# A transformer block and a hybrid block on one core: ScalarE and VectorE kept in the order of emission, and a row's store put behind its sum of squares

## The chip, the core and the metric

The kernel runs on one core of one Trainium2 chip. Five engines work side by side: TensorE (PE in the profile; PEld is its weight load), VectorE (DVE), ScalarE (ACT), GpSimd (POOL) and SyncE (SP), which here mostly issues DMAs. Each engine takes its own list of instructions, and waits for the others by semaphores. The metric is the device time of one execution in microseconds (us), lower is better; the median over several runs counts.

## The reference

1024 rows of width 1024 in float32 go through two blocks.

```
# first block
x = x + 0.5 * rms_norm(swiglu(rms_norm(x), w_gate, w_up, w_down))      # FFN1, inner width 2816
x = x + rms_norm(token_mixer(rms_norm(x)))                             # 8 heads with forget gates, 4 differential heads
x = x + 0.5 * rms_norm(swiglu(rms_norm(x), w_gate, w_up, w_down))      # FFN2
# second block, on 16 learned rows + the 1024 rows
h = h + mixed(RG-LRU, SSD)(rmsnorm(h)) @ w_out                         # even layer: two recurrences with short convolutions
h = h + stick_breaking(rmsnorm(h)) @ w_out                             # odd layer: 16 heads, cumulative sums instead of softmax
return rmsnorm(h)[16:]
```

## The kernel before

**Stages.** FFN1 runs to about 700 us of the span, the mixer to 1300, FFN2 to 1990, the even layer to 2760, and the odd layer to the end. Every product is made of three passes over operands that are split into a high and a low part (`mm3`: high by high, low by high, high by low). So each operand of TensorE needs two earlier steps: ScalarE casts the high part (`wh`, `w0h`, `T`, `th`, `Ah`: a `copy` to fp32r), and VectorE subtracts it from the source for the low part (`wl`, `w0l`, `tl`, `Al`). The two FFNs use a scheme with fewer products of larger sums: VectorE forms the sums (`sg` L826, `w` L785), and `T3`, `T4` are split sums of the activations. DMAs are issued from SP's queue, and the stores of finished rows from ScalarE's queue (L607).

**Two orders.** The class `Sched` (L109 to L198) is the kernel's own planner: threads ask for time on an engine with a cost (`("A", act(n))`, `("V", dve(n))`, ...), and the thread that can start first by these costs is served, so it decides the order in which instructions are emitted. The framework below the kernel (Tile) then has a scheduler of its own, which takes ready instructions by its own estimates and may place an instruction of any engine before others that were emitted earlier. In the kernel before only loads of activation tables and the activations `act_t` are tied to each other (`pin`, `last`, `after_pin`). By count, 1141 of VectorE's instructions and 557 of ScalarE's stand directly behind one that was emitted later.

**Names of the steps below.** At the start, `Start.half` squares four rows `xr` on ScalarE for their sums (`ss`), VectorE computes 1/sqrt (`rsqrt`, 12 small operations L287 to L294) and scales the rows (`norm`, L626); TensorE transposes them (`ptf`, L577), and `Ah`, `Al` (L565) are the split of the result; `w0h`, `w0l` are the first weights. `ahead_of` (L508 on) prepares `w_out` of a later stage during FFN1: eight blocks `prer` come by DMA, are cast on ScalarE, subtracted on VectorE (L520), and go back to DRAM. In the even layer `xc` is a convolution (L2550, L2553), and L2766 to L2770 make the decay blocks `ab` of a chunk, eight small operations. In the odd layer `kt` is a scan (L2275), `pt` the weights that come from it (L2279), `th` and `tl` (L1552) the split of their transposes, which TensorE multiplies with the values into `po` (L1587). `Rows.put` takes one finished row tile: store it to DRAM, square and sum it.

Of the kernel before, what the change touches and what calls it, by code (L numbers as in the profile page):

```python
# [12 lines left out]
AF = mybir.ActivationFunctionType  # L13
# [5 lines left out]
P = 128  # L19
# [21 lines left out]
class Res:  # L41


    def __init__(self, n):
        self.free = [0.0] * n
        self.queue = []
# [50 lines left out]
def act(n):  # L97
    return 0.07 + 0.92e-3 * n
# [102 lines left out]
class Ctx:  # L201
    def __init__(self, ctx, tc):
        self.ctx = ctx
        self.tc = tc
        nc = self.nc = tc.nc
        self.sch = Sched(self.act_set)
        self.const = ctx.enter_context(tc.tile_pool(name="const", bufs=1))
        self.small = ctx.enter_context(tc.tile_pool(name="small", bufs=4))
        self.ap = ctx.enter_context(tc.tile_pool(name="act", bufs=1))
        self.wp = ctx.enter_context(tc.tile_pool(name="W", bufs=1))  # L210
        self.psp = None
        self.ahead = None
        self.dr = ctx.enter_context(tc.tile_pool(name="dr", bufs=1, space=DRAM))
        self.ident = self.const.tile([P, P], F32, name="ident")
        make_identity(nc, self.ident)
        self.eps = self.const.tile([P, 1], F32, name="epsc")
        nc.vector.memset(self.eps, EPS)
        self.one = self.const.tile([P, 1], F32, name="onec")
        nc.vector.memset(self.one, 1.0)
        self.pin = None  # L220
        self.last = None
        for nm in ("activation", "copy"):
            def f(*a, _o=getattr(nc.scalar, nm), **k):
                self.last = _o(*a, **k)  # L224
                return self.last
            setattr(nc.scalar, nm, f)
        self.onesm = self.const.tile([P, P], F32, name="onesm")
        nc.vector.memset(self.onesm, 1.0)

    def new_A(self):  # L230
        return (self.ap.tile([P, KD, L], F32R, tag="Ah", name="Ah"),
                self.ap.tile([P, KD, L], F32R, tag="Al", name="Al"))

    def after_pin(self, ins):

        if self.pin is not None:
            self.tc.add_manual_dep(ins.ins, self.pin.ins.name, mybir.DependencyInfo(
                mybir.DependencyClass.NoSync, mybir.DependencyReason.DATA), reason="table set")
        return ins

    def act_set(self, name):

        ins = self.after_pin(self.nc.scalar.preload_act_table_set(name))
        if self.last is not None and self.last is not self.pin:
            self.tc.add_manual_dep(ins.ins, self.last.ins.name, mybir.DependencyInfo(
                mybir.DependencyClass.NoSync, mybir.DependencyReason.DATA), reason="table set")
        self.pin = ins

    def act_need(self, name):

# [332 lines left out]
class Rows:  # L583
# [15 lines left out]
    def put(self, t, y, junk):  # L599

        c, g = self.c, self.GROUP[t]
        ms = self.members(t)
        if g not in self.ss:
            self.ss[g] = c.small.tile([P, len(ms)], F32, tag=f"ss{len(ms)}", name="ss", bufs=5)
        if self.dram is not None:
            r0 = self.row0 + t * P
            c.nc.scalar.dma_start(self.dram[r0:r0 + P, :], y)  # L607
        tt = yield ("A", act(1024))
        c.nc.scalar.activation(junk(), y, AF.Square, accum_out=self.ss[g][:, t - g:t - g + 1])
        self.stored[t].set(tt + 3.0)  # L610
        self.left[g] = self.left.get(g, len(ms)) - 1
        if self.left[g] == 0:
            if t >= self.tables:
                self.r[g] = yield from c.rsqrt_t(self.ss[g], 1.0 / D)
                tt = c.sch.time
            else:
                tt = yield ("V", c.RSQRT)
                self.r[g] = c.rsqrt(self.ss[g], 1.0 / D)
            for u in ms:
                self.ev[u].set(tt)  # L620
# [2688 lines left out]
```

## Time and profile before

| | |
|---|---|
| median of 3 runs (lowest to highest) | 3579.32 us (3578.43 to 3579.59) |
| the profiled execution's own time | 3577.13 us |
| its span, first to last instruction | 3575.4 us |
| TensorE busy | 3430.7 us, 96% |
| VectorE busy | 2749.9 us, 77% |
| ScalarE busy | 1700.6 us, 48% |
| mean granted TensorE clock, of full speed | 0.987 |

The profile is of one execution. [...]

### The profile page before, as it was taken

How to read it: one execution, taken by the hardware profiler on the slowest of the kernel's cores; microseconds unless marked ns; L12 is line 12 of the kernel's file. 1: busy time of each engine (PE TensorE's matmuls, PEld its weight loads, DVE VectorE, ACT ScalarE, POOL GpSimd, SP SyncE). 2: the span in 40 equal slices, each digit the busy share in tenths (PEclk: the TensorE clock that was granted, in tenths of full speed). 3: DMA queues.
4: the chain of work that ended last, by engine and by line, in shares of the span. 5: the costliest groups of instructions: out<-in, count | busy, mean ns of one | idle time of the engine just before them, and what ended most of it. 6: DMA issues, size and time to landing. Idle time of an engine off the chain costs nothing.

```text
span 3575.4 us, 51885 instructions
## 1 busy us (share of the span) xinstructions
PE 3430.7 (96%) x19675; PEld 2925.6 (82%) x19675; DVE 2749.9 (77%) x5050; ACT 1700.6 (48%) x3451; POOL 326.1 (9%) x355
## 2 busy tenths in 40 slices
PE   8999999899999999999999899998999999999998
PEld 6788888678888877888888899988878888888877
DVE  8876699988888769666799779578633688878784
ACT  5323245556666643232345447447422465656561
POOL 0111144000000001111351000000000000000000
PEclk9999999999999999999999999999999999999999
DMA  5542372311211551323552334244473110111133
GB/s 183 178 132 89 113 284 83 128 58 44 73 41 36 179 168 60 123 89 109 195 197 72 108 64 86 61 87 90 139 244 95 57 36 28 33 31 31 33 134 107
DMA packets 305842, 366.07 MB, mean 102 GB/s; under 512 B 18644, under 2 KB 221568, under 8 KB 305592
## 3 DMA queue, kind: packets, MB, share of 16 engines
q1 hardware_dynamic: 299800, 341.71, 30.7%
q10 hardware_dynamic: 5792, 21.04, 1.6%
q8 instruction: 155, 2.54, 0.3%
q14 instruction: 95, 0.78, 0.1%
HBM read 267.58 MB, written 95.13 MB: 101 GB/s over the span
## 4 chain that ended last, share of the span: by engine, by line
PE 73%; DVE 17%; ACT 4%; issue 3%; DMA 2%; SPq 0%; POOL 0%; DVEq 0%; ACTq 0%; POOLq 0%
PE pst L337 7%; PE pst L336 7%; PE pst L338 7%; PE po L1587 3%; PE pe L336 3%; PE pe L338 3%; PE pe L337 3%; DVE kt L2275 3%; PE pdn L337 2%; PE pdn L338 2%; PE pdn L336 2%; PE ptr L1607 2%; PE pwo L3100 2%; PE pwo L3101 2%; PE pwo L3102 2%
## 5 line engine op out<-in xcount | busy, mean ns | idle before, releaser
L336 PE MATMUL pe<-Ah,wh 128*128 128x260 f32 (+1 forms) x1184 | 340.6, 288 | 21.9 <-DVE sz L2601 8.2
L338 PE MATMUL pe<-Ah,wl 128*128 128x260 f32 (+1 forms) x1184 | 337.1, 285 | 0.0
L337 PE MATMUL pe<-Al,wh 128*128 128x260 f32 (+1 forms) x1184 | 336.4, 285 | 0.0
L224 ACT CAST wh<-w 128x512 fp32r<-128x512 f32 x280 | 162.1, 619 | 252.7 <-PE pst L337 160.2
L942 DVE TENSOR_TENSOR sg<-sg,pst 128x512 f32<-128x512 f32 x280 | 187.1, 684 | 104.8 <-PE pst L338 104.4
L1006 POOL TENSOR_TENSOR h<-h 128x512 f32<-128x512 f32 x88 | 136.2, 1547 | 1332.9 <-DVE h L988 1327.7
L337 PE MATMUL pst<-Al,wh 128*128 128x512 f32 x640 | 253.7, 396 | 0.0
L336 PE MATMUL pst<-Ah,wh 128*128 128x512 f32 x640 | 252.2, 394 | 0.0
L338 PE MATMUL pst<-Ah,wl 128*128 128x512 f32 x640 | 252.1, 394 | 0.0
L473 DVE TENSOR_TENSOR wl<-w,wh 128x512 fp32r<-128x512 f32 x280 | 212.0, 784 | 50.4 <-ACT wh L224 49.0
L336 PEld LDWEIGHTS pe<-Ah,wh 128*128 128x128 f32 (+1 forms) x1184 | 223.4, 189 | 26.2 <-DVE sz L2601 8.5
L337 PE MATMUL pdn<-dl,dh 128*128 128x512 f32 x592 | 230.8, 390 | 1.9 <-DVE dl L1099 1.9
L224 ACT CAST th<-ptr 128x512 fp32r<-128x512 f32 (+2 forms) x344 | 171.6, 515 | 125.4 <-PE ptr L1607 78.7
L338 PE MATMUL pdn<-dh,dl 128*128 128x512 f32 x592 | 230.3, 389 | 0.0
L1552 DVE TENSOR_TENSOR tl<-ptr,th 128x512 fp32r<-128x512 f32 (+2 forms) x344 | 197.5, 592 | 41.8 <-ACT th L224 38.4
L336 PE MATMUL pdn<-dh 128*128 128x512 f32 x592 | 229.1, 389 | 0.0
L337 PEld LDWEIGHTS pe<-Al,wh 128*128 128x128 f32 (+1 forms) x1184 | 223.0, 189 | 1.0
L338 PEld LDWEIGHTS pe<-Ah,wl 128*128 128x128 f32 (+1 forms) x1184 | 222.8, 188 | 0.8
L2275 DVE TENSOR_TENSOR_SCAN kt<-kt,onec 128x392 f32<-128x392 f32 (+5 forms) x224 | 204.2, 916 | 16.8 <-ACT kt L224 14.9
L224 ACT CAST wh<-wr 128x1024 fp32r<-128x1024 f32 (+2 forms) x116 | 119.0, 1026 | 182.7 <-PE pwo L3101 80.3
L336 PE MATMUL pst<-T,wh 128*128 128x512 f32 x480 | 187.3, 393 | 8.7 <-ACT T L224 8.7
L337 PE MATMUL pst<-T,wh 128*128 128x512 f32 x480 | 188.1, 392 | 0.4 <-DVE T L835 0.4
(550 smaller groups left out, 10023.6 us busy)
## 6 DMA issues: line engine op xcount, KB each, us to landing
hD<-h SPq DMA_DIRECT2D x22, 1792.0 KB, 8.1
w<-in_ffn_w_gate_dram SPq DMA_DIRECT2D x20, 1024.0 KB, 5.4
w<-in_ffn_w_up_dram SPq DMA_DIRECT2D x20, 1024.0 KB, 8.0
d<-hD SPq DMA_DIRECT2D x18, 1024.0 KB, 5.4
wr<-in_even_w_in_dram SPq DMA_DIRECT2D x36, 512.0 KB, 4.3
wo<-prer SPq DMA_DIRECT2D x32, 512.0 KB, 3.6
wr<-in_odd_w_in_dram SPq DMA_DIRECT2D x32, 512.0 KB, 4.3
wr<-in_w_in_dram SPq DMA_DIRECT2D x24, 512.0 KB, 3.9
```

What stands on the lines that cost most here:

```text
L224: self.last = _o(*a, **k)
L336: nc.tensor.matmul(ps, wh, xh, start=start, stop=False)
L337: nc.tensor.matmul(ps, wh, xl, start=False, stop=False)
L338: nc.tensor.matmul(ps, wl, xh, start=False, stop=stop)
L473: (nc.gpsimd if eng == "G" else nc.vector).tensor_sub(lo, raw, hi.bitcast(F32))
L942: nc.vector.tensor_add(dst, src, ps)
L1006: nc.gpsimd.tensor_sub(q[:, o], q[:, a], q[:, b_])
L1552: nc.vector.tensor_sub(tl[:rows, :n], ptr[:rows, :n], th[:rows, :n].bitcast(F32))
L1587: nc.tensor.matmul(po[:, 256 - n:256], vs, (th, tl)[w][:rows, o:o + n], start=(x == 0 and y == 0 and 0 in which), stop=(x == last and y == ...
L1607: nc.tensor.transpose(ptr[:rows, o:o + P], pts[i][:, col:col + rows], c.ident)
L2275: nc.vector.tensor_tensor_scan(rev, rev, c.one.to_broadcast([P, m]), kt[:, k0 + m:k0 + m + 1], op0=ALU.mult, op1=ALU.mult)
L3100: nc.tensor.matmul(ps[n], oh, wh[:, sl], start=(first and k == 0), stop=False)
```

## The change

Every `activation` and `copy` of ScalarE, every table load, and fourteen kinds of VectorE operation are tied to the instruction of the same engine that was emitted before, by a dependency that needs no semaphore, since both stand in one engine's list. TensorE, GpSimd and SP are not tied. In `Rows.put` the store is emitted after the Square and tied behind it. Nothing is added to or taken from the computation.

```diff
@@ class Ctx, __init__
+        self.inner = False
...
         self.pin = None
         self.last = None
-        for nm in ("activation", "copy"):
-            def f(*a, _o=getattr(nc.scalar, nm), **k):
-                self.last = _o(*a, **k)
-                return self.last
-            setattr(nc.scalar, nm, f)
+        self.tail = {}
+        self.strict = True
+
+        def record(e, ins):
+            if e == "A":
+                self.last = ins
+            if e in self.tail:
+                self.behind(ins, self.tail[e])
+            if self.strict:
+                self.tail[e] = ins
+            return ins
+
+        self.record = record
+        for e, eng, names in (("A", nc.scalar, ("activation", "copy")), ("V", nc.vector, (
+                "memset", "reciprocal", "reduce_sum", "scalar_tensor_tensor", "stream_shuffle", "tensor_add",
+                "tensor_copy", "tensor_mul", "tensor_reduce", "tensor_scalar", "tensor_sub", "tensor_tensor",
+                "tensor_tensor_reduce", "tensor_tensor_scan"))):
+            for nm in names:
+                def f(*a, _o=getattr(eng, nm), _e=e, **k):
+                    was, self.inner = self.inner, True
+                    ins = _o(*a, **k)
+                    self.inner = was
+                    return ins if was else record(_e, ins)
+                setattr(eng, nm, f)
...
+    def behind(self, ins, first):
+
+        self.tc.add_manual_dep(ins.ins, first.ins.name, mybir.DependencyInfo(
+            mybir.DependencyClass.NoSync, mybir.DependencyReason.DATA), reason="order of emission")
...
@@ act_set
-        self.pin = ins
+        self.pin = self.record("A", ins)
...
@@ Rows.put
+        tt = yield ("A", act(1024))
+        c.nc.scalar.activation(junk(), y, AF.Square, accum_out=self.ss[g][:, t - g:t - g + 1])
         if self.dram is not None:
             r0 = self.row0 + t * P
-            c.nc.scalar.dma_start(self.dram[r0:r0 + P, :], y)
-        tt = yield ("A", act(1024))
-        c.nc.scalar.activation(junk(), y, AF.Square, accum_out=self.ss[g][:, t - g:t - g + 1])
+            c.behind(c.nc.scalar.dma_start(self.dram[r0:r0 + P, :], y), c.last)
```

By count, 96 of VectorE's instructions and 2 of ScalarE's now stand directly behind one that was emitted later. In the rows below, wrapped instructions carry the wrapper's line: L224 of ScalarE before, L243 of both engines now.

The first place is ScalarE at the start of FFN1, before:

```order
L224 ACT_TABLE_LOAD
L224 ACTIVATE junk,ss<-xr 128x1024 x4
L224 CAST w0h<-wr 128x1024 x2
L224 CAST w0h<-w_139 128x1024
L224 CAST w_149<-w_139 128x1024
L224 ACTIVATE Ah<-ptf,prm_95 128x512 x4
```

And with the change:

```order
L243 ACT_TABLE_LOAD
L243 ACTIVATE junk,ss<-xr 128x1024 x2
L243 CAST w0h<-wr 128x1024 x2
L243 ACTIVATE junk,ss<-xr 128x1024 x2
L243 CAST w0h<-w_139 128x1024
L243 CAST w_149<-w_139 128x1024
L243 CAST wh<-w 128x512
L243 ACTIVATE Ah<-ptf,prm_95 128x512 x8
```

The Squares of the second two rows (`junk,ss<-xr`) moved behind the casts of the first weights `w0h`. VectorE's order moved alike: the two `w0l` and the second rsqrt chain now stand ahead of the first two scalings of rows, and the four scalings stand together.

The second place is ScalarE in FFN1 at about 100 us, where `T3_643` and `T4_901` are split sums that TensorE waits for and `prer` belongs to the preparation of `w_out`; before:

```order
L224 CAST T3_643<-sg_803 128x512
L224 CAST wh_828<-w_180 128x512
L224 CAST wh_828<-w_219 128x512
L224 CAST wh_870<-w_180 128x512
L224 CAST wh_870<-w_219 128x512
L224 CAST prer_1687<-prer_1686 128x1024
L224 CAST T3_643<-sg_848 128x512
L224 CAST wh_928<-w_180 128x512
L224 CAST wh_928<-w_219 128x512
L224 ACTIVATE sg_909<-sg_909 128x512
L224 CAST T4_901<-sg_903 128x512
L224 CAST prer_1865<-prer_1864 128x1024
```

And with the change:

```order
L243 CAST T3_643<-sg_803 128x512
L243 CAST wh_870<-w_180 128x512
L243 CAST wh_870<-w_219 128x512
L243 CAST T3_643<-sg_848 128x512
L243 ACTIVATE sg_909<-sg_909 128x512
L243 CAST T4_901<-sg_903 128x512
L243 CAST wh_928<-w_180 128x512
L243 CAST wh_928<-w_219 128x512
L243 CAST T4_901<-sg_904 128x512
```

The `prer` casts left this place; `prer_1687` now stands about 70 instructions behind the last `T3_643`, and the subtractions of `prer` on VectorE moved back likewise.

The third place is VectorE in the odd layer, where `tl_27237` and `tl_27255` are what TensorE's `po` products wait for, and `wl_27244` is a weight's low part for a later projection; before:

```order
L2279 TENSOR_TENSOR pt_27197<-pt_27197,kt_27204 128x392
L2275 SCALAR_TENSOR_TENSOR kt_27204<-kt_27204,onec_76 128x392
L2279 TENSOR_TENSOR pt_27197<-pt_27197,kt_27204 128x392
L473 TENSOR_TENSOR wl_27244<-wr_27093,wh_27243 128x1024
L1552 TENSOR_TENSOR tl_27237<-ptr_27235,th_27236 128x256
L1552 TENSOR_TENSOR tl_27255<-ptr_27253,th_27254 128x512
L2275 SCALAR_TENSOR_TENSOR kt_27257<-kt_27257,onec_76 128x456
L2226 TENSOR_TENSOR g1_27023<-g1_27023,pg_27118 128x512
```

And with the change:

```order
L243 TENSOR_TENSOR pt_27197<-pt_27197,kt_27204 128x392
L243 TENSOR_TENSOR tl_27237<-ptr_27235,th_27236 128x256
L243 SCALAR_TENSOR_TENSOR kt_27204<-kt_27204,onec_76 128x392
L243 TENSOR_TENSOR tl_27255<-ptr_27253,th_27254 128x512
L243 TENSOR_TENSOR pt_27197<-pt_27197,kt_27204 128x392
L243 SCALAR_TENSOR_TENSOR kt_27257<-kt_27257,onec_76 128x456
...
L243 TENSOR_TENSOR pt_27325<-pt_27325,kt_27326 128x352
L243 TENSOR_TENSOR wl_27244<-wr_27093,wh_27243 128x1024
```

The two `tl` moved ahead of a scan, a `pt` and `wl_27244`, and `wl_27244` now stands 13 instructions behind `tl_27237`.

## Rows read from the trace of the kernel before

**Rows 1.** The page: busy time of each engine.

```profile
PE 3430.7 (96%) x19675; PEld 2925.6 (82%) x19675; DVE 2749.9 (77%) x5050; ACT 1700.6 (48%) x3451; POOL 326.1 (9%) x355
```

**Rows 2.** Busy time by stretches: the five stages, and 10 us of FFN1.

```profile
core 0: us, PE busy (x) PEld busy (x) DVE busy (x) ACT busy (x) POOL busy (x), PEclk, DMA share, GB/s
...
103.20:113.40 10.20, 7.00 (x15) 4.70 (x16) 10.20 (x17) 4.47 (x7) 0.00 (x0) 0.50 0.42 154
...
0.00:700.00 700.00, 670.00 (x2930) 547.16 (x2931) 577.11 (x875) 283.24 (x497) 152.62 (x93) 0.99 0.43 146
700.00:1300.00 600.00, 583.04 (x3488) 489.14 (x3487) 491.23 (x1290) 354.62 (x875) 1.04 (x2) 0.99 0.25 82
1300.00:1990.00 690.00, 669.60 (x2935) 546.92 (x2934) 558.35 (x839) 267.94 (x476) 146.86 (x80) 0.99 0.37 125
1990.00:2760.00 770.00, 741.28 (x5393) 674.73 (x5393) 499.30 (x902) 358.65 (x576) 7.64 (x38) 0.98 0.41 108
2760.00:3475.00 715.00, 675.73 (x4523) 593.85 (x4521) 573.37 (x1003) 417.12 (x991) 17.96 (x142) 0.99 0.14 45
```

**Rows 3.** Waits of TensorE, whole span: us in total, times, longest.

```profile
PE pst L336 <- ACT T L224: 8.7, 4, 4.0
PE pe L336 <- DVE sz L2601: 8.2, 1, 8.2
PE psx L2747 <- ACT xc L224: 7.2, 1, 7.2
...
PE ptf L577 <- DVE gp L626: 6.4, 2, 3.2
PE pe L336 <- DVE Al L565: 6.2, 1, 6.2
...
PE pd L336 <- DVE Al L565: 4.8, 1, 4.8
...
PE pe L336 <- ACT xb L224: 3.5, 1, 3.5
```

**Rows 4.** Waits of TensorE in the odd layer, 2760 to 3475 us.

```profile
PE po L1587 <- DVE tl L1552: 21.3, 28, 2.8
PE po L1587 <- ACT th L224: 8.1, 10, 1.3
```

**Rows 5.** ScalarE's timeline at 100 us: start, duration, [idle before].

```profile
101.36 1.04 ACT L224 CAST prer<-prer 128x1024 fp32r<-128x1024 f32 x1 [4.22 <-DMA prer<-in_w_out_dram]
103.61 0.62 ACT L224 CAST T<-sg 128x512 fp32r<-128x512 f32 x1 [1.21 <-DVE sg L826]
```

**Rows 6.** ScalarE's timeline at the start.

```profile
10.82 1.05 ACT L224 CAST w0h<-wr 128x1024 fp32r<-128x1024 f32 x1 [0.61 <-DMA wr<-in_ffn_w_gate_dram]
12.63 1.04 ACT L224 CAST w0h<-wr 128x1024 fp32r<-128x1024 f32 x1 [0.76 <-DMA wr<-in_ffn_w_up_dram]
```

**Rows 7.** VectorE's timeline at the start.

```profile
7.05 0.17 DVE L287 TENSOR_SCALAR rs_v<-ss 128x2 f32<-128x2 f32 x1 [5.63 <-ACT junk L224]
...
9.31 0.15 DVE L294 SCALAR_TENSOR_TENSOR rs_y<-rs_a,rs_y 128x2 f32<-128x2 f32 x1
...
15.23 1.42 DVE L626 TENSOR_SCALAR xr<-xr,rs_y 128x1024 f32<-128x1024 f32 x2
...
18.83 2.72 DVE L565 SCALAR_TENSOR_TENSOR Al<-ptf,prm,Ah 128x512 fp32r<-128x512 f32 x4
```

**Rows 8.** The start of FFN2: TensorE's first product, and ScalarE's last Square of a row.

```profile
1312.52 0.77 PE L336 MATMUL pgu<-Ah,w0h 128*128 128x512 f32 x1
...
1317.20 1.06 ACT L224 ACTIVATE pt<-y 128x1024 f32<-128x1024 f32 x1
```

**Rows 9.** VectorE's timeline at the end of FFN1.

```profile
669.20 2.48 DVE L1252 SCALAR_TENSOR_TENSOR acc<-acc,rs_y,gp 128x1024 f32<-128x1024 f32 x2
```

**Rows 10.** VectorE's timeline in the even layer.

```profile
2345.05 1.66 DVE L2770 TENSOR_SCALAR ab<-ab,dT 128x128 f32<-128x128 f32 x8
```

**Rows 11.** VectorE's timeline in the odd layer.

```profile
2935.69 1.22 DVE L473 TENSOR_TENSOR wl<-wr,wh 128x1024 fp32r<-128x1024 f32 x1
```

## The prediction

> **What bounds the kernel now.** I read the page first: TensorE is busy 3430.7 us of a span of 3575.4 [rows 1], so 144.7 us are all that any better order of the other engines can win directly. VectorE at 77% and ScalarE at 48% have room over the whole, so the question is where TensorE stands still and for whom. By stages [rows 2] its idle time is 30.0 us in FFN1 (700.00 - 670.00), 17.0 in the mixer, 20.4 in FFN2, 28.7 in the even layer and 39.3 in the odd one. The view of waits [rows 3] shows single waits of 3 to 8 us in the first four stages: for `T`, `gp`, `Al`, `xb`, `xc` and `sz`, which ScalarE or VectorE write. In the odd layer it is 38 short waits for `tl` and `th`, 21.3 + 8.1 = 29.4 us [rows 4]. Waits cost a second time: for 10.20 us behind the wait for `T3` the granted clock is 0.50, the lower of the two levels, with TensorE busy for 7.00 of them [rows 2]; at full clock that work takes half, 3.5 us less.
>
> The profiled execution took 3577.13 us, 1.7 more than its span and 2.2 less than the median of the runs. I sum on 3577.13 and add 2.2.
>
> **What the change moves.** No instruction of TensorE, ScalarE or VectorE is added or removed that does work, and the order costs no semaphore, so the price is only in who stands behind whom. I went through the places where TensorE waits, and through those where an instruction that it needs moved back. Plus is slower.
>
> *Start of FFN1, +4.8.* Two Squares now stand behind the two `w0h` casts, which wait for DMAs; the second cast starts at 12.63 and lasts 1.04 [rows 6]. Two Squares of 1.06 [rows 8], with about 0.2 each to read the sum, end at about 16.3. The rsqrt chain took from 7.05 to 9.46 (9.31 + 0.15) [rows 7], 2.4 us, so 18.7. All four scalings now stand behind it, 2 x 1.42 [rows 7]: 21.5. Two weight splits like the `wl` of 1.22 [rows 11] follow: 23.9, less the overlap of neighbours, about 23.7. There `Al` starts, at 18.83 before [rows 7]. Nothing covers it, TensorE has no other product yet: 23.7 - 18.8 = 4.9, and I take 4.8. If the casts' DMAs come no later, the bounds are 3 and 6.
>
> *T3 and T4 in both FFNs, -5.8.* ScalarE waits 4.22 us for the DMA of a `prer`, casts it at 101.36 for 1.04, and the cast of `T3` comes next, at 103.61 [rows 5]. TensorE's four waits for `T` sum to 8.7 [rows 3]. The `prer` casts and the subtractions of 1.2 us on VectorE leave this stretch, so that the `T` splits have 4 to 8 us less in front of them. What stays is about 1.5 in FFN1, for a quarter of `T3` whose low part moved back by 3.9 us of VectorE's work, and as much in FFN2: 8.7 - 2.9 = 5.8. Bounds: 0, if `sg` is what is late, and -8.7.
>
> *Start of FFN2, +3.* TensorE's first product there began at 1312.52 and needs `w0h`; that cast stood some 30 us ahead, and now stands behind the last Square of a row, which starts at 1317.20 and takes 1.06 [rows 8]. Cast and split, 1.05 and 1.2, end at about 1320.2, 7.7 us after the product wants them. Of that, waits for rows that TensorE has there anyway are swallowed, and the product's other operands come first; I take 3, bounds 0 and 7.7.
>
> *Ends of the FFNs, 0 each.* The last product's splits, which had been done early, now stand behind the closing chain of the finished rows, six operations of about 1.24 (2.48 for two [rows 9]), 7.5 us, and have a cast (0.62 for 512 columns [rows 5]) and a subtraction of their own: some 9 us of new waiting. But the waits that come next, for `gp` and `Al` (half of 6.4, and 4.8 and 6.2 [rows 3]), 8 to 10 us, are for the results of that same chain, which has then been done. One replaces the other: 0, with bounds of -6 and +6 each.
>
> *Mixer, 0.* Here the order of TensorE's own instructions changes too; about 8 us of its waits lose what stood before them, and about 8 come where inputs moved back. Bounds -8 and +8, about half of the 17.0 [rows 2].
>
> *Even layer, -8.* The decay blocks, 1.66 for eight [rows 10] and 2.0 with their two small companions, had been put ahead as soon as their DMA was there, and now stand just before their use, 20 to 45 us of work later. Two of them stood before the convolution behind the wait of 7.2 for `xc`: -4. The wait of 3.5 for `xb` has a decay block and a `wl` before it and goes: -3.5. Before the `sz` of the wait of 8.2 stand 3.8 us less: -3.8 [rows 3]. That is -11.3; weights `wh` and `wl` that had been made early now come later, in about three places of 1.2 [rows 11], +3.3. Bounds -12 and +4.
>
> *Odd layer, -18.* At the place shown, `tl_27237` stood behind a scan and a `wl` of 1.22 [rows 11] that now follow it. Counted so at all 51 stops of TensorE in this stage, each at the lesser of its wait and of the work that leaves its producer's queue, 28.9 us go. What moved back is asked for in its turn: the `wl` (1.22) and `wh` of the next projections and the splits of the queries, some eight times. I charge 11 for that, a good 1.2 us each, by the row of the `wl`. Bounds -27, hardly anything comes back, and 0, all of it comes back.
>
> *Store behind the Square, +2.* The store starts one Square later, 1.06 [rows 8] and the reading of the sum; four rows of each stage are loaded again from that store, and TensorE waits for them at the stage's turn. Three turns, at most 3.7 in all; I take 2, and 0 where the load is hidden.
>
> *Clock, -4.* The stretch at 103.20 is 3.5 [rows 2]; the larger waits of the even layer keep 3 to 4 us each, so their slow stretches are mostly left. Bounds -12 and +5.
>
> **Sum:** 4.8 - 5.8 + 3 + 0 + 0 - 8 - 18 + 2 - 4 = -26.0; 3577.1 - 26.0 = 3551.1 in the profile, 3553.3 in the median.
>
> [...]
>
> **Rivals.**
>
> *Blocked queues (slower).* The planner's costs are not the chip's, and where an input is late, the whole engine stops. The place where that decides is the end of each FFN: if the last splits wait for the closing chain and the waits for `gp` and `Al` stay, because the chain then starts later too, each end costs 9 instead of 0, +18. The odd layer has the same pattern: a `tl` whose transposes come late now holds back the scans behind it, so that its gain falls to -4. -26 + 18 + 14 = +6, and up to +18 where the scans lose all their lead and the clock drops with the new waits: 3585 to 3598. It decides once more than 26 us of waits are new. For it speaks that VectorE had been free to fill in 1141 places; against it that ScalarE and VectorE idle for much of every stage [rows 2].
>
> *The odd layer's waits only move (no change).* If `th`, `tl`, scans and `pt` are a loop paced by VectorE, a `tl` that goes ahead of a scan delays the next `pt`, and TensorE waits there. Then the odd layer gives 0: -26 + 18 = -8, and with half of the other gains lost about 3572 to 3585. For it: in this layer VectorE is busy 573.37 of 715 [rows 2], the scans among it. Against: 20% of idle time is room enough for 38 waits of 0.8 us on average (29.4 / 38 [rows 4]).
>
> *More than counted (much faster).* If the emitted order is close to one without waits, the odd layer gives 27, the even 12, the mixer 8, the FFN ends 6, the clock 12, and the other terms as above (-5.8, +4.8, +3, +2): -61, so 3518.
>
> **Chances.** The likeliest, 3553 with 3535 to 3571 as its own range (the odd layer's term at -27 or -9, and one FFN end either way): 0.50. Much faster, under 3535: 0.13. Moved waits: 0.17. Blocked: 0.20. Within 0.2%, 7 us, is about what a measurement here can't tell from no change: 3572 to 3586. Of the moved waits 0.10 lie in it and 0.07 below, of the blocked 0.02 in it. So faster 0.70, same 0.12, slower 0.18. The range 3516 to 3600 takes in the bounds of the rivals.
>
> **What would show it.** In the profile after: the first `Al` at about 23.7 instead of 18.83; no wait of 4 us for `T` at 104 and full clock behind it; TensorE's idle time in the odd layer from 39 to about 21, with `tl` and `th` far down in the view of waits; a wait for the splits of the last product near 667 and none for `gp` after it; the wait for `xc` at about 3 instead of 7.2. It is wrong if TensorE waits in the odd layer for scans, `pt` or weights as long as for `tl` before, or if the FFN ends show both the old waits and the new.

## The result: 3712.81 us, 3.7% slower

The change takes 3712.81 us in the median (3709.89 to 3713.69, 4 runs), beside 3578.88 for the kernel before on the same chip: a ratio of 1.0373, 95% interval 1.036 to 1.0386. That is outside the range on record (3516 to 3600) and on the other side of the forecast.

The page of the profile after, its line of busy times, answers to [rows 1]; the span is 3708.1 us:

```profile
PE 3480.5 (94%) x19675; PEld 2959.8 (80%) x19675; DVE 2854.5 (77%) x5050; ACT 1709.3 (46%) x3451; POOL 339.7 (9%) x355
```

TensorE's idle time has grown from 144.7 to 227.6 us (3708.1 - 3480.5), by 82.9. Its busy time has grown by 49.8 with the same 19675 instructions: the mean granted clock, a share of full speed, fell from 0.987 to 0.971, and more of the work ran at 0.5, the lower of the two levels (1.0 and 0.5) that the clock records of both traces have. 82.9 + 49.8 is the whole difference of the spans, 132.7.

The stages stand later by what was lost before them, so they are cut at nearly the same instructions. This view of stretches of the kernel after answers to the five stages of [rows 2]:

```profile
core 0: us, PE busy (x) PEld busy (x) DVE busy (x) ACT busy (x) POOL busy (x), PEclk, DMA share, GB/s
0.00:714.00 714.00, 674.36 (x2924) 548.88 (x2925) 606.58 (x868) 283.14 (x491) 158.04 (x91) 0.99 0.42 143
714.00:1360.00 646.00, 604.95 (x3495) 503.47 (x3494) 510.64 (x1292) 355.71 (x879) 2.09 (x4) 0.96 0.24 76
1360.00:2067.00 707.00, 675.78 (x2944) 548.38 (x2944) 593.18 (x830) 268.31 (x471) 151.22 (x80) 0.98 0.36 121
2067.00:2870.00 803.00, 748.20 (x5381) 679.62 (x5380) 515.52 (x913) 362.67 (x584) 9.44 (x38) 0.96 0.40 106
2870.00:3601.00 731.00, 679.25 (x4504) 599.71 (x4503) 576.86 (x1002) 417.63 (x988) 18.90 (x142) 0.97 0.14 44
```

TensorE's idle time (first number less the second) is 39.6, 41.1, 31.2, 54.8 and 51.8 us, where it was 30.0, 17.0, 20.4, 28.7 and 39.3. The mixer and the even layer lost most, and their clock fell from 0.99 and 0.98 to 0.96. Not one stage has gained.

The longest waits of TensorE after, over the whole span (us in total, times, longest), stand in place of [rows 3]:

```profile
PE po L1612 <- DVE tl L243: 31.3, 38, 2.6
PE psy L2831 <- DVE ab L243: 21.0, 5, 8.7
PE pdn L362 <- DVE dl L243: 17.5, 10, 5.1
PE pe L361 <- DVE sz L243: 15.1, 3, 10.1
PE psc L1565 <- ACT pt L243: 12.7, 12, 3.5
PE ptf L602 <- DVE xr L243: 9.4, 1, 9.4
...
PE ptf L602 <- DVE Al L243: 7.1, 4, 2.6
PE pe L361 <- ACT sz L243: 6.9, 1, 6.9
```

The waits for `xc`, `xb` and `gp` are gone or small, as forecast. But `tl` has as much as before, and `ab`, `dl`, `sz`, `pt` and `xr` are new or larger.

**Where the time went** is seen best by following single instructions of TensorE. Two of them in the mixer, the products `psc` of one block of scores, before:

```profile
855.49 0.44 PE L1540 MATMUL psc<-ks('d', 1)1_6373,qs 128*128 128x512 f32 x1
855.77 0.40 PE L1541 MATMUL psc<-ks('d', 1)1_6373,qs 128*128 128x512 f32 x1
```

And the same two after:

```profile
882.90 0.45 PE L1565 MATMUL psc<-ks('d', 1)1_6373,qs 128*128 128x512 f32 x1
883.18 0.39 PE L1566 MATMUL psc<-ks('d', 1)1_6373,qs 128*128 128x512 f32 x1
```

Here TensorE is 27.4 us late. Taking this lateness for all its instructions (paired in the order of emission) and its growth between places of the program gives the table at the end of the next section, from one profiled execution each; without a cause it wanders by 1 to 3 us in places, and a total by up to about 6 (the run with the store alone, whose median is that of the kernel before, has +5.7). For the change it reads: +5.4 at the start, +11.6 and +11.8 at the ends of the two FFNs, +41.9 in the mixer, +11.7 at the start of FFN2, +26.8 in 90 us of the even layer, +16.1 and +8.4 at the start and end of the odd layer, and -0.9 in its steady part.

### The profile page after: what moved, and what is told of

Read it like the earlier page. It is cut to its first block, busy times and chain, and to the rows that moved or that the text cites. A ratio compares the mean times of both kernels' runs of the same rounds, so it can differ in the third digit from the quotient of the medians.

```text
span 3708.1 us, 51919 instructions
## 1 busy us (share of the span) xinstructions
PE 3480.5 (94%) x19675; PEld 2959.8 (80%) x19675; DVE 2854.5 (77%) x5050; ACT 1709.3 (46%) x3451; POOL 339.7 (9%) x355
## 3 DMA queue, kind: packets, MB, share of 16 engines
q1 hardware_dynamic: 299800, 341.71, 29.7%
## 4 chain that ended last, share of the span: by engine, by line
PE 72%; DVE 19%; ACT 4%; issue 3%; DMA 2%; POOL 0%; SPq 0%; DVEq 0%; ACTq 0%
PE pst L362 6%; PE pst L361 6%; PE pst L363 6%; PE pe L361 3%; PE pe L363 3%; PE pe L362 3%; PE po L1612 3%; DVE kt L243 3%; PE pdn L362 3%; PE pdn L363 3%; PE pdn L361 3%; PE ptr L1632 2%; DVE dl L243 2%; DVE pt L243 2%; PE pwo L3125 2%
## 5 line engine op out<-in xcount | busy, mean ns | idle before, releaser
L361 PE MATMUL pe<-Ah,wh 128*128 128x260 f32 (+1 forms) x1184 | 340.7, 288 | 26.8 <-DVE sz L243 15.1
L243 DVE TENSOR_TENSOR sg<-sg,pst 128x512 f32<-128x512 f32 x280 | 186.8, 684 | 126.1 <-PE pst L363 124.3
L1031 POOL TENSOR_TENSOR h<-h 128x512 f32<-128x512 f32 x88 | 147.2, 1673 | 1379.0 <-DVE h L243 1373.9
L243 ACT CAST th<-ptr 128x512 fp32r<-128x512 f32 (+2 forms) x344 | 170.5, 514 | 187.2 <-PE ptr L1632 135.6
L243 ACT CAST wh<-w 128x512 fp32r<-128x512 f32 x280 | 161.0, 617 | 203.1 <-PE pst L362 82.1
L243 DVE TENSOR_TENSOR wl<-w,wh 128x512 fp32r<-128x512 f32 x280 | 229.5, 855 | 15.3 <-ACT wh L243 13.9
L243 DVE TENSOR_TENSOR tl<-ptr,th 128x512 fp32r<-128x512 f32 (+2 forms) x344 | 197.7, 592 | 47.7 <-ACT th L243 44.7
L243 DVE TENSOR_TENSOR_SCAN kt<-kt,onec 128x392 f32<-128x392 f32 (+5 forms) x224 | 205.1, 916 | 15.5 <-ACT kt L243 14.2
L363 PE MATMUL pst<-T,wl 128*128 128x512 f32 x480 | 188.2, 392 | 0.0
```

The costliest lines, as they stand in the source:

```text
L243: ins = _o(*a, **k)
L361: nc.tensor.matmul(ps, wh, xh, start=start, stop=False)
L363: nc.tensor.matmul(ps, wl, xh, start=False, stop=stop)
L1031: nc.gpsimd.tensor_sub(q[:, o], q[:, a], q[:, b_])
```

## The experiments

Theories. A: an instruction whose input is late stands at the head of a fixed list and holds up ready ones. B: urgent results stand behind other work that was emitted earlier, and work that had been done far ahead now stands on the path. C: it is the later store. D: it is TensorE's own list, which the framework still sets and which no longer fits. All diffs are against the changed kernel; differences are against the kernel before, measured beside it.

**One part alone.** Only ScalarE tied, or only VectorE (with `"V"`):

```diff
-            if e in self.tail:
+            if e in self.tail and e == "A":
                 self.behind(ins, self.tail[e])
```

> Only ScalarE keeps the order of emission (with the store behind the Square); VectorE is placed freely again. Theory A (an instruction whose input is late stands at the head of a fixed list and holds up ready ones; ScalarE's list has the most of them: DMA-fed weight casts and casts of transposes that TensorE still has to make): half or more of the 134 us stays, 3640 to 3690. Theory B (what costs is VectorE's filler work, which no longer floats forward and now stands just before its use): VectorE has 2937 + 1092 of the moved instructions, so ScalarE's list alone costs little, 3580 to 3610. Theory C (it is the store): as with the store alone.

> Only VectorE keeps the order of emission (with the store behind the Square); ScalarE is as before. Theory A: VectorE's instructions mostly follow a cast of ScalarE, which now comes as early as it can; less than half stays, 3590 to 3640. Theory B: nearly all stays, 3680 to 3715. Theory C: as with the store alone.

3650.76 us, +71 (ratio 1.0199, 1.0184 to 1.0214), and 3727.45, +147 (1.0418, 1.0401 to 1.0436). Each list costs by itself. VectorE's alone costs a little more than both, which A didn't expect and which lies 12 us above B's range; ScalarE's alone costs half, which B didn't.

No ties, only the store behind its Square:

```diff
-            if e in self.tail:
-                self.behind(ins, self.tail[e])
```

> Neither engine is tied, only the store of a row is emitted and tied behind its Square. Theories A and B: the store is one Square of 1.06 us later at three turns of stages, of which the sum on record took 2 us: 3576 to 3584. Theory C (the later store delays the rows that the next stage reads back, and the long waits at the turns, 8 us near 700, 12 us near 1380, 15 us near 2800 are from it): 3600 to 3615, and more with the fixed lists.

3579.77 beside 3579.97 (1.0002, 0.9993 to 1.0012). C is out: the store costs nothing by itself.

**More freedom.** Each instruction tied to the n-th before it, n = 8, 2 and 32:

```diff
-            if e in self.tail:
-                self.behind(ins, self.tail[e])
-            if self.strict:
-                self.tail[e] = ins
+            line = self.tail.setdefault(e, [])
+            if len(line) == 8:
+                self.behind(ins, line.pop(0))
+            line.append(ins)
```

> Each instruction of ScalarE and VectorE is tied to the eighth one emitted before it instead of the last, so that the framework may exchange close neighbours but can't float work forward by tens of microseconds. Theory A (late heads, overtaken by near neighbours that are ready): most of the loss goes, 3560 to 3610. Theory B (what matters is far-floating filler work): most of the loss stays, 3650 to 3710.

> As the change, but each instruction is tied to the second one emitted before it. If the mixer loses because next neighbours in the fixed lists become ready in the other order, a freedom of one place gives back a third to a half of its 42 to 45 us and of the whole 134: 3645 to 3675. If longer exchanges are needed, 3690 to 3715.

> As the change, but each instruction is tied to the thirty-second one emitted before it. If the rest of the loss at a freedom of eight (53 us: turns of the stages, decay blocks in the last chunks of the even layer) is work that had been done far ahead, 32 places, some 20 us of VectorE's work, give back most of it: 3575 to 3595, and the wait for T near 100 us stays won. If it is the ties as such, 3615 to 3635.

3631.58, +52 (1.0149, 1.0134 to 1.0164); 3675.93, +99 (1.0273, 1.0254 to 1.0291); 3581.74, +4.5 (1.0012, 1.0002 to 1.0022). With 1, 2, 8 and 32 places the loss is 134, 99, 52 and 4.5 us; the run with eight falls between the two theories, the run with two just outside what was expected of next neighbours. In the mixer the loss is 41.9, 32.1, 8.4 and 0.3: exchanges over a few places are what is missing there. At the turns of the stages and in the last chunks of the even layer eight places give back a third to two thirds, and 32 most: there it is also work that had been done far ahead.

**Classes of instruction left out of the ties** (a flag makes the wrapper return early):

```diff
+            if self.loose:
+                return ins
             if e in self.tail:
                 self.behind(ins, self.tail[e])
...
+        c.loose = True
         nc.scalar.copy(hi, raw)
+        c.loose = False
```

First the splits of weights (as above in `split` and `ahead_of`), then those of the transposes (`th`, `tl` in `pt_evac`):

> As the change, but the casts and subtractions that split weights (fed by DMA: wh, wl, w0h, w0l, prer) are left out of the ties on both engines; all other instructions keep the order of emission. Theory A (weights whose DMA is late stand at the head of a list): the single large places go (27 us in the even layer near 2500 of the span before, 10 at the start of FFN2, 5 at the start of FFN1), and with them 60 or more of the 134 us: 3590 to 3655. Theory B (urgent results of the computation itself stand behind other work that was emitted earlier, in the mixer above all): the weights are little of it, 3670 to 3710. Theory D (TensorE's own list, which the framework still sets, no longer fits the fixed lists): hardly any change.

> As the change, but the splits of transposed attention weights (th on ScalarE, tl on VectorE, which wait for TensorE's transposes) are left out of the ties. Theory A in the mixer (ScalarE waits 79.3 us at th for TensorE, twice what it did before, and holds up the exponentials): some 25 of the 45 us of the mixer go, 3680 to 3695. Theory B: th and tl then float in front of more urgent reductions, and little is won, 3700 to 3720. Theory D: hardly any change.

3694.24, +118 (1.0325, 1.031 to 1.034), and 3706.25, +130 (1.0358, 1.0343 to 1.0374). B's numbers held in both, though "hardly any change", as D had it, fits the second as well. With the weights free the loss is 16 us less: the start of FFN2 and the start and end of the odd layer gain 5.8, 8.5 and 8.9, and two stretches (up to 480 and up to 2480) lose 5.2 and 6.9 more. With the transposes free it is hardly less.

**TensorE tied as well:**

```diff
-                "tensor_tensor_reduce", "tensor_tensor_scan"))):
+                "tensor_tensor_reduce", "tensor_tensor_scan")), ("P", nc.tensor, ("matmul", "transpose"))):
```

> As the change, with TensorE's matmuls and transposes tied in the order of emission as well, so that all three engines follow the planner. Theory D (the loss comes from TensorE's list, placed by other estimates than the two fixed ones): half or more of the 134 us goes, 3580 to 3650. Theories A and B: the planner's order itself has the waits, and TensorE now has late heads too, 3700 to 3760.

3788.02, +212 (1.0584, 1.0568 to 1.06). So the loss doesn't come from TensorE leaving the planner's order: what freedom its list has left saves 78 us. That the framework's list for TensorE is as good beside the tied engines as it was before is not shown by this. It did change: paired as above, TensorE has another instruction in front in 443 of 3486 places of the mixer, but in only 15 of 5392 of the even layer (22 and 3 in the run with the store alone). In the even layer its order can hardly be a cause; in the mixer its share is not separated.

**The gains of the forecast by themselves.** No ties but for `prer` (both engines) and the decay blocks, each tied behind the instruction emitted before it, with nothing tied behind them (the flag stands around the casts and subtractions of `prer` and around `dec` in the same way):

```diff
-            if e in self.tail:
+            if self.follow and e in self.tail:
                 self.behind(ins, self.tail[e])
...
+                c.follow = True
                 nc.vector.tensor_scalar(m[:, h], m[:, h], acT[:, h:h + 1], 0.0, op0=ALU.subtract, op1=ALU.min)
+                c.follow = False
```

> Neither engine is tied, except that the filler work on which the sum on record put gains (prer in FFN1, the decay blocks of the even layer) may not stand ahead of the instruction that was emitted before it. If those two terms were right as such and only the rest of the order lost, this gives -4 to -5 near 100 us and -4 to -8 in the even layer: 3567 to 3574. If the fillers cost nothing where they stood, 3577 to 3583.

3584.05, a ratio of 1.0017 (1.0007 to 1.0026), outside both bounds. The table has both gains, -3.5 in FFN1 and -3.5 in the even layer, and a loss of 14.6 near its end. TensorE's waits between 2470 and 2545 us of this run:

```profile
PE psy L2840 <- DVE ab L244: 14.7, 3, 7.4
```

In these waits TensorE does nothing else, and a decay block that is made just before its use puts the chain of block, exponential, product on the path. So another run ties the decay blocks in the first group of nine only (`c.follow = g == 0`):

> As the run with only the fillers tied, but the decay blocks are tied in the first of their two groups of nine alone, where the wait of 3.5 us for xb had gone, and free in the second, where two waits of 7 us had come. Theory B: -2.5 near 100 us and -3 to -5 in the first group stay, the 14.6 us of the second group don't come: 3569 to 3575, the first kernel here below the kernel before. If the two waits come from anything else than the tied blocks, 3580 to 3586.

3568.89 beside 3576.01, a ratio of 0.9974 (0.9963 to 0.9985): the one kernel here that is faster than the kernel before. Its waits of TensorE from 0 to 120 us have

```profile
PE pst L362 <- ACT T L244: 3.1, 2, 1.9
```

where the longest was 4.0 [rows 3], and the table has -3.5, -3.9 and no loss at the end.

**Urgent work left out of the ties:** the minima `mx` over fresh scores in the mixer, and the decay blocks, by the flag `loose`:

> As the change, but VectorE's minimum over fresh scores in the mixer (the mx reductions, on which the exponentials wait) and the decay blocks of the even layer are left out of the ties. Theory B (urgent results stand behind work that was emitted earlier; work that was done early now stands on the path): the mixer's 42 us shrink to 15 to 30, and of the 27 us in the even layer near 2500 of the span before 12 or more go, so 3660 to 3685. Theory A (late heads alone, whoever stands behind): less than 12 in both, 3695 to 3710.

3738.21, +162 (1.0448, 1.0433 to 1.0462), worse than the change; both theories missed. The mixer gave back 9 of 42 us. The even layer, up to 2480, lost 36.3 where the change has -0.8. VectorE's waits there (2100 to 2680 us) have

```profile
DVE dec L246 <- DMA ab<-aD: 58.3, 18, 6.0
```

and those of the kernel before, from 2030 to 2560 us,

```profile
DVE dec L2766 <- DMA ab<-aD: 29.7, 14, 5.3
```

The free decay blocks went to the front, where their DMA had not landed, and all that is tied stood behind them. That fits A, in one place. But half of such waiting was there before, in an order that could put other work ahead of it, so the length of the waits alone is not the price.

**One stage alone:** the ties switched on in `tile_network_kernel` around `mixer_stage`, and from `odd_stage` on.

```diff
-            if e in self.tail:
+            if self.on and e in self.tail:
                 self.behind(ins, self.tail[e])
...
+    c.on = True
     odd_stage(c, A4, rows4, prm, odd_w_in_2[0], wo2, h1,
```

> Both engines keep the order of emission in the mixer alone. Theory B (the order inside the mixer is what loses there, whatever came before): +35 to +50, 3615 to 3630. If the loss was inherited from stages that came late before it: under +15, 3580 to 3595.

> Both engines keep the order of emission in the odd layer alone. The term of the sum on record, -18, would give 3562. By the shift of TensorE's instructions in the run of the change it is 0 in the steady part, +10 to +15 at its start and +5 to +8 at its end: 3593 to 3603. If start and end were inherited from the even layer's lateness: 3575 to 3583.

3624.47, +48 (1.0127, 1.0113 to 1.0141), and 3599.55, +24 (1.0063, 1.0048 to 1.0078). Both losses are the stage's own and hardly inherited; of the 16.1 at the start of the odd layer 11.1 come so.

The growth of TensorE's lateness against the kernel before, in us, between the places of the program that stood at these times of its span; columns are named by their end, the last is the total:

```
run               60     480     720    1290    1480    2030    2480    2570    2840    3450    3570   total
the change      +5.4    +0.7   +11.6   +41.9   +11.7   +11.8    -0.8   +26.8   +16.1    -0.9    +8.4  +132.7
e1_act_only     +6.6    -4.5    +5.6   +17.9    +6.9    +8.1    +2.4    +6.2   +12.9    -0.6    +6.1   +67.6
e2_dve_only     +4.5    +0.7    +9.1   +47.9   +13.9   +12.4    +3.2   +26.9   +16.1    +8.4    +6.1  +149.3
e3_store_only   +1.9    -0.1    -1.2    +1.4    -0.4    +1.2    +2.6    +0.1    -0.1    +0.6    -0.2    +5.7
e13_slack2      +4.3    +0.0   +11.3   +32.1   +10.2   +12.7    -4.3   +20.9   +10.9    -2.5    +5.7  +101.3
e4_slack8       +1.3    -3.8    +6.3    +8.4    +4.5    +4.2    -1.7   +17.7    +8.8    +2.0    +5.7   +53.3
e14_slack32     +0.3    -3.9    +0.1    +0.3    +4.2    +2.2    -8.3    +8.2    +0.9    -0.6    +2.7    +6.2
e5_weights_free +2.9    +5.9   +11.7   +40.8    +5.9   +11.6    +6.1   +23.0    +7.6    +1.6    -0.5  +116.5
e6_trans_free   +5.6    +0.6   +11.8   +40.7    +9.4   +11.4    -0.3   +26.8   +14.8    +1.7    +5.8  +128.3
e7_pe_tied      +6.4    +9.5   +13.3   +72.2   +19.9   +14.4    +4.1   +27.6   +16.4   +15.2    +9.7  +208.7
e8_fillers      +1.2    -3.5    -0.2    +0.1    -0.1    +0.5    -3.5   +14.6    -1.9    +0.7    -0.3    +7.6
e9_urgent_free  +4.6    +1.9   +11.8   +33.2   +12.6   +12.3   +36.3   +25.6   +14.3    -0.6    +7.5  +159.5
e10_fillers_g0  +0.1    -3.5    -0.0    -0.1    -0.1    +0.7    -3.9    +0.1    -2.4    -0.5    -1.1   -10.9
e11_mixer_only  -0.3    -0.2    +2.0   +43.1    +1.9    +0.9    +2.4    -0.0    -0.0    -1.1    -0.5   +48.2
e12_odd_only    +0.6    +0.1    -0.3    -1.5    +0.7    -0.5    +1.0    -0.0   +11.1    -0.6    +7.9   +18.6
```

## Why the prediction was wrong

**The step that failed** is the way of counting: "each at the lesser of its wait and of the work that leaves its producer's queue", and on the other side a price for those inputs alone that moved back. That prices the places where TensorE waited before. It has no term for the places where it did not wait because the framework had put whatever was ready next. A fixed list loses there in two ways, which the runs with 2, 8 and 32 places separate: among near neighbours, where no instruction moves far enough to show as a moved input (the mixer, 41.9 us with one place, 8.4 with eight), and where work that had been done far ahead was cover (the turns of the stages and the last chunks of the even layer). The rival "blocked queues" had the direction and named late heads, but priced them at the two FFN ends and part of the odd layer, up to +18 us in all. It was +134.

**Start of FFN1, +4.8: right.** ScalarE's timeline after has the second pair of Squares behind the DMA-fed casts:

```profile
12.12 1.04 ACT L243 CAST w0h<-wr 128x1024 fp32r<-128x1024 f32 x1 [0.76 <-DMA wr<-in_ffn_w_up_dram]
13.07 1.05 ACT L243 ACTIVATE junk<-xr 128x1024 bf16<-128x1024 f32 x1
```

VectorE starts `Al` at 22.61 (23.7 forecast), and TensorE is 5.4 late; what it waits for is the scaled rows (`xr`, 9.4 above), not `Al`. At the start of FFN2 the term was +3, and the waits for `w0h` and `w0l` there are 3.3 and 1.4, so it was right in itself. But TensorE lost 11.7 up to 1480, with waits for `Al` of 5.5 (1.0 before) and for `T` of 4.6 (3.0 before); without the weights in the ties it lost 5.9.

**T3 and T4, -5.8: the gain is there without the rest, but by VectorE, and not in the change.** With `prer` alone tied, or ScalarE alone, FFN1 gains 3.5 to 4.5. The forecast's reading of [rows 5] doesn't hold, though: the `prer` cast that waited for its DMA ended at 102.40, and the cast of `T` then waited 1.21 us more for `sg`, so nothing that was ready stood behind it. In the run with `prer` and the first nine decay blocks tied, the same cast comes 2.8 us earlier and still waits for `sg`:

```profile
100.80 0.62 ACT L244 CAST T<-sg 128x512 fp32r<-128x512 f32 x1 [3.59 <-DVE sg L244]
```

VectorE, which makes `sg`, has no idle time here (10.20 of 10.20 us [rows 2]), and it is its subtraction of `prer` that left the place; before:

```profile
92.73 1.23 DVE L520 TENSOR_TENSOR prer<-prer 128x1024 fp32r<-128x1024 f32 x1
```

In the change VectorE's list has other work in the same place, five sums of later weights ahead of the low part of `T`:

```profile
105.81 3.10 DVE L243 TENSOR_TENSOR w<-w 128x512 f32<-128x512 f32 x5
108.82 0.69 DVE L243 TENSOR_TENSOR T<-sg,T 128x512 fp32r<-128x512 f32 x1
```

TensorE waits 4.6 us for it. I had taken away what left the queue, and had not looked at what else was emitted ahead.

**Ends of the FFNs, 0 with bounds of 6: wrong,** +11.6 and +11.8, but not by the trade that the term priced. At the end of FFN1 TensorE's timeline after has

```profile
691.02 0.80 PE L362 MATMUL pdn<-dl,dh 128*128 128x512 f32 x1 [5.11 <-DVE dl L243]
...
704.63 0.80 PE L361 MATMUL pd<-Ah,wh 128*128 128x512 f32 x1 [3.38 <-DVE Al L243]
723.47 0.60 PE L361 MATMUL pg<-Ah,wh 128*8 128x512 f32 x1 [4.69 <-ACT rx L243]
```

The last split (`dl`) does wait behind the closing chain, and the waits for that chain's results shrink: 5.1 for `dl`, 1.1 for `acc` and 3.4 for `Al` stand beside 3.2 for `gp` and 4.8 for `Al` before, 9.6 beside 8.0. In FFN2 it is 9.2 (5.1, 1.4, 2.7) beside 9.4. What had no term lies on both sides: the splits of the products ahead of it (`dl` and `dh`, 4.2 and 5.3 us in the two FFNs, where it was 0.9 and 1.0), and the first inputs of the next stage (`rx` 4.7, before 0.5; behind FFN2 `x1r` 5.1 in three waits, before none).

**Mixer, 0 with bounds of 8: wrong by 42.** At the `psc` shown above, the minimum over these scores ran before at

```profile
856.81 0.68 DVE L1966 TENSOR_REDUCE mx<-psc 128x1 f32<-128x512 f32 x1
```

0.64 us after the product's end (855.77 + 0.40). After, VectorE's timeline has

```profile
886.14 1.23 DVE L243 TENSOR_TENSOR wl<-wr,wh 128x1024 fp32r<-128x1024 f32 x1
887.28 0.42 DVE L243 TENSOR_SCALAR rw_a<-pss 128x256 f32<-128x256 f32 x1
887.80 0.88 DVE L243 TENSOR_TENSOR rw_a<-rw_a,rw_y 128x256 f32<-128x256 f32 x2
...
890.17 1.27 DVE L243 TENSOR_REDUCE mx<-psc 128x1 f32<-128x512 f32 x2
```

The scores were there at 883.57 (883.18 + 0.39) and the minimum starts 6.6 us later, behind a weight's split and the normalization of another head. The exponentials need the minima of both halves of the block, though. The end of the second half's scores and the first exponential, before:

```profile
859.00 0.23 PE L1543 MATMUL psc<-mask_up,identb 128*128 128x128 bf16 x1
...
860.58 0.69 ACT L224 ACTIVATE pt<-psc,mx 128x512 f32<-128x512 f32 x1
```

And after:

```profile
887.65 0.23 PE L1568 MATMUL psc<-mask_up,identb 128*128 128x128 bf16 x1
...
891.67 0.69 ACT L243 ACTIVATE pt<-psc,mx 128x512 f32<-128x512 f32 x1 [2.85 <-DVE mx L243]
```

From the end of these scores to the exponential it takes 1.35 us before (860.58 - 859.23) and 3.79 after (891.67 - 887.88): of the 6.6 us, 2.4 reach the path here. The exponentials free the buffers of scores, and TensorE's next product of scores waits:

```profile
892.50 0.58 PE L1565 MATMUL psc<-ks('f', 0)0_6616,qs 128*128 128x256 f32 x1 [3.51 <-ACT pt L243]
```

VectorE was busy for 6.25 of the 6.60 us from 883.57 to 890.17: ready urgent work behind ready work that could wait. Freeing the minima gave 9 us in the mixer, eight places of freedom 33: it is not this class alone but the order among neighbours. That this one place is typical of the rest is not shown.

**Even layer, -8: wrong by 34.** Of the early gains (-11.3 in the forecast) -3.5 came with the fillers alone tied, where the waits for `xb` and `xc` fell to 1.7 and 5.4 and that for `sz` grew to 10.4; in the change the waits for `xb` and `xc` all but went, but `sz` took 15.1 instead of 8.2, and -0.8 was left. Against this stand 26.8 us near its end, where VectorE's timeline after shows a late head:

```profile
2589.72 0.68 DVE L243 TENSOR_TENSOR xe<-xd,dec 128x512 f32<-128x512 f32 x1
2594.50 1.23 DVE L243 TENSOR_TENSOR wl<-wor,wh 128x1024 fp32r<-128x1024 f32 x1 [4.09 <-ACT wh L243]
2595.64 1.22 DVE L243 TENSOR_TENSOR ab<-ab,cbm 128x1024 f32<-128x1024 f32 x1
```

ScalarE's cast for that `wl` waited for a DMA, the product `ab` that TensorE needs stood behind, and TensorE waited:

```profile
2593.42 1.04 ACT L243 CAST wh<-wor 128x1024 fp32r<-128x1024 f32 x1 [2.52 <-DMA wor<-in_even_w_out_dram]
...
2596.91 1.98 PE L2831 MATMUL psy<-ab,xd 128*64 128x128 f32 x16 [8.67 <-DVE ab L243]
```

With weights free that wait is 4.25, but the stretch still loses 23.0, so the late head is the smaller part. The next wait of 7.5 is the decay block that is no longer made ahead, which the run with the fillers alone shows by itself (+14.6).

**Odd layer, -18: wrong by 42.** In the steady part TensorE's waits for `tl` and `th` were to lose 28.9 us. After, from 2870 to 3615 us:

```profile
PE po L1612 <- DVE tl L243: 27.2, 32, 2.6
PE pv L1550 <- ACT wh L243: 4.6, 4, 1.4
PE pq L361 <- ACT wh L243: 3.0, 1, 3.0
...
PE po L1612 <- ACT th L243: 2.4, 2, 2.2
```

For `tl` and `th` that is 29.6 us, beside 29.4 [rows 4]: the rival "the waits only move" was right for this part, at -0.9. The start and the end of the layer, on which no term stood, cost 16.1 and 8.4, and with weights out of the ties 7.6 and -0.5. At the start TensorE waits for weights itself (the `wh` of `pq`, 3.0, and one of the four for `pv`). At the end (from 3570 us) its waits are for `tl`, 5.9 where they were 3.4, so that how the weights delay it there is not shown.

**Store, +2:** 0. **Clock, -4:** the wrong sign. By the clock records of the two traces TensorE was busy for 66 us at the lower level before and for 157 us after. In the kernel before, products of 128x512 start 0.43 us apart at a clock of 0.50 (from 111.07 to 112.78 us) and 0.23 us apart at 1.00 (from 114.46 to 115.38), about half; so half of the difference, some 45 us, is an estimate of what it took of the 49.8.

What stays open: which exchanges in the mixer matter, beyond that they are short; and why VectorE's ties alone cost more than both together (47.9 against 41.9 in the mixer, +8.4 against -0.9 in the steady odd layer).

## What to carry to other kernels

A fixed order is only as good as the costs it was planned with: before tying an engine to it, count not just the waits that the ties would remove but how often the scheduler now overtakes (1141 places here), since each is a place where a tied list can wait. If some filler work does harm where it floats, tie that filler alone, behind what was emitted before it and with nothing behind it; that was the one gain here (0.26%), and it too had to leave out the chunks in which the early work was cover. A tie to the 32nd instruction before kept the far work back (-3.9 up to 480, -8.3 up to 2480) and cost 4.5 us in all.

## What the runs showed of the hardware

In these runs waiting cost TensorE more than its own length: with ties of 1, 2 and 8 places its idle time rose by 82.9, 58.5 and 36.4 us, and its busy time, with the same 19675 instructions, by 49.8, 42.8 and 16.9, at a mean granted clock of 0.971, 0.976 and 0.983, where the kernel before has 0.987. In the stretch of three long waits that begins with the 8.67 us for `ab` above (7.50 and 6.90 us follow), the profile after has a clock of 0.57:

```profile
2590.00:2625.00 35.00, 13.68 (x74) 11.74 (x75) 18.41 (x40) 10.47 (x17) 0.00 (x0) 0.57 0.15 50
```

Where the instruction that VectorE took next waited for a DMA, VectorE stood still: for 58.3 us in 18 waits for the decay blocks in the run with these free, and for 29.7 us in 14 in the kernel before.
